# Two fused transformer blocks: PSUM pairs from two pools, an earlier scaling of x, and two modulation vectors summed on VectorE

## The chip, the core and the metric

The kernel runs on one core of a Trainium2 chip. The metric is device time in microseconds (us), the median of several runs. One more execution of the same program was taken with the hardware profiler; all rows below are from it.

## The reference

The input x has 256 tokens of 2048 features. It goes through two blocks, each with a conditioning vector c. All arithmetic is to float32 accuracy.

```python
# block 1
mod = silu(c) @ w_ada + b_ada                       # six vectors of 2048: sh_m, sc_m, gt_m, sh_f, sc_f, gt_f
h = rmsnorm(x, pre_mix_norm) * (1 + sc_m) + sh_m
proj = h @ w_in                                     # HGRN2 (q, f, v, g) and gated DeltaNet (q, k, v, g, a, b) columns
y = concat(hgrn2(proj), gated_delta(proj)) @ w_out
x = x + gt_m * rmsnorm(y, post_mix_norm)
h = rmsnorm(x, pre_ffn_norm) * (1 + sc_f) + sh_f
y = square(relu(h @ w_ff1)) @ w_ff2
x = x + gt_f * rmsnorm(y, post_ffn_norm)
# block 2: the same frame with its own six vectors, four kinds of attention and a SwiGLU; then a last rms_norm
```

What matters here is the first lines: each of the six vectors of a block is one row of `silu(c) @ w_ada`, a product of a single row with a 2048x2048 slice of a weight matrix (16 MB), and the first product `h @ w_in` needs vectors 0 and 1, the second norm needs 3 and 4.

## The kernel before

**Weights.** Every weight arrives in items of 512 KB ("raw", 128x1024). ScalarE rounds an item to the reduced float32r format (wh), VectorE (in some later stages GpSimd) takes the rest (wl = raw - wh, L169 as all instructions, since a helper issues them), and TensorE multiplies the activations, split likewise into hTh and hTl, in three passes: h*wh, h*wl, l*wh. There are four slots for split items and five raw slots (eight in the early rounds). SyncE's queue issues the loads in the order of a list, `items`; an item is loaded when a raw slot comes free.

**Order.** The program is one straight list for each engine. Python code writes it with the help of a planner, `_Clock`, which adds up assumed costs for each instruction: `fill()` is called after each pair of k-tiles and issues evacuations (`pri`), modulation vectors (`urgent`), steps of the recurrences and of attention (`fillers`; not if VectorE's planned time is more than 12 us ahead of TensorE's) and the preparation of further items (`prep`).

**Modulation vectors.** The items of `ADA` lie between the weight items. There are two ways to do them. With `cg=True` (vectors 0 to 4 of block 1) TensorE does them: `ada_cg` takes two items, and four matmuls at a time write the four 32-row strips of one bank ("ada", 128*32 in the profile); ScalarE or VectorE takes the 128x512 bank over into an "acc" tile. The others (vector 5 of block 1, all of block 2) are done on VectorE: acc = raw * silu(c) + acc, with silu(c) as a scalar of each partition, 128x512 at a time, two for an item. `col_gen` then sums an acc over its partitions into columns A and B of a norm (AB["mix1"], AB["ffn1"], ...): in block 1 by matmuls with a column of ones, in block 2 by transposes and ScalarE sums. `row_gen` spreads a gate vector over all partitions. There are four acc tiles of 128x512; `room` forces waiting vectors out when they are taken.

**Start and early rounds.** First come the 16 items of the first quarter of vectors 0 and 1. Meanwhile x arrives, `x_pre` sums its squares, and `xnT_gen(q)` scales 512 columns on ScalarE, transposes them through TensorE and copies them by ScalarE. Then the first 12 k-tiles of the eight `wide` blocks (hq, hf, hv, hg, zq, zk, zv, gg of the first half) are done in three rounds of four k-tiles, since each quarter of vectors 0 and 1 opens four k-tiles of h (`first_hT`). hq and hf keep their two PSUM banks ("g", four banks) over all rounds. The six others take a pair of the pool "mx" (three banks) in each round, and it is emptied into SBUF partial sums (hv, hg and "part") after each: in round one by ScalarE and VectorE, then by `add_acc` on VectorE. `xnT_gen(1)` to `(3)` follow the first three blocks of round one. The rest of the projections with the recurrences (`hg_gen`, `gd_gen`), vectors 3, 4 and 2 and the output projection (oA, oB) come after.

The evacuation of the second half's hq waits until the first half's `hg_gen` is done, and that of the second half's zq, zk and zv until the first half's `gd_gen` is.

Of the kernel before, what the change touches and what calls it, by code (L numbers as in the profile page):

```python
# [9 lines left out]
F32 = mybir.dt.float32  # L10
# [9 lines left out]
D = 2048  # L20
# [158 lines left out]
def two_blocks(ctx, tc, I, out):  # L179
# [21 lines left out]
    accp = ctx.enter_context(tc.tile_pool(name="acc", bufs=4))  # L201
# [35 lines left out]
    def add_ada(blk, v, q, kp, fin, row, cg):  # L237
        items.append({"ada": (blk, v, q, kp), "fin": fin, "row": row, "cg": cg})

    def room(n):  # L240
        for _ in range(40):
            if len(accs) + n > 4:
                fill_step(True, urgent)

    def dma_to(n):
        while st["d"] < min(n, len(items)) and rslots:
# [5 lines left out]
            if "ada" in it:  # L252
                blk, vs, q, kp = it["ada"]
                c0 = vs[0] * D + q * 512
                w = adas[blk][0]
                if kp == 0 and (it["row"] or not it["cg"]):
                    room(len(vs))
                    for v in vs:
                        a = accp.tile([128, 512], F32, name="acc", tag="acc")
                        accs[blk, v, q] = a  # L260
                        if it["row"]:
                            pool.memset(a, 0.0)
                            sync.dma_start(a[0:1, :], adas[blk][1][c0:c0 + 512].rearrange("(o n) -> o n", o=1))
                if len(vs) == 1:
                    src = w[kp * 256:(kp + 1) * 256, c0:c0 + 512].rearrange("(k p) n -> p k n", p=128)
                else:
                    src = w[kp * 128:(kp + 1) * 128, vs[0] * D:(vs[1] + 1) * D].rearrange("p (v n) -> p v n", v=2)[:, :, q * 512:(q + 1) * 512]
# [6 lines left out]
    def prep(low=None):  # L274
# [9 lines left out]
        if "ada" in it:  # L284
            blk, vs, q, kp = it["ada"]
# [34 lines left out]
    def ada_cg(it):  # L320

        blk, (v,), q, kp = it["ada"]
        cgs.setdefault("held", []).append(it)
        if kp % 2:
# [3 lines left out]
            for j in range(4):  # L328
                i = cgs["held"][j // 2]
                kt = blk * 16 + 2 * i["ada"][3] + j % 2  # L330
                mm(p[32 * j:32 * j + 32], csil[:, kt:kt + 1].to_broadcast([128, 32]),
                   i["raw"][:, (j % 2) * 512:(j % 2 + 1) * 512], kp == 1, kp == 7)
# [4 lines left out]
        if kp == 7:  # L337
            if it["row"]:
                a = accs[blk, v, q]
                dve.scalar_tensor_tensor(a, p, 1 / 32, a, op0=MUL, op1=ADD)  # L340
            else:
                room(1)
                a = accs[blk, v, q] = accp.tile([128, 512], F32, name="acc", tag="acc")
# [352 lines left out]
    def col_gen(blk, v, q):  # L696
        a = accs.pop((blk, v, q))
        name = (("mix1", "ffn1"), ("mix2", "ffn2"))[blk][v // 3]
        p = mx()
        if blk == 0:  # L700
# [20 lines left out]
    def row_gen(blk, v, q, key, mul):  # L721
# [5 lines left out]
        a = accs.pop((blk, v, q))  # L727
# [20 lines left out]
    def ada_vecs(blk, vs, key=None, mul=False, cg=False):  # L748
        n = 8 * len(vs)
        for q in range(4):  # L750
            for kp in range(n):
                fin = None
                if kp == n - 1:
                    if key is None:
                        fin = lambda q=q: urgent.extend((clk.wr[clk.key(accs[blk, v, q])][0] + 0.2, col_gen(blk, v, q)) for v in vs)
                    else:
                        fin = lambda q=q: urgent.append((clk.wr[clk.key(accs[blk, vs[0], q])][0] + 0.2, row_gen(blk, vs[0], q, key, mul)))
                ADA.append((blk, vs, q, kp, fin, key is not None, cg))
# [1588 lines left out]
```

## Time and profile before

| | us |
|---|---|
| median of 3 runs | 2887.93 |
| lowest and highest | 2885.76, 2890.27 |
| the profiled execution | 2885.77 |
| its span, first to last instruction | 2883.8 |

The profile counts, for every engine, the time in which it executes ("busy"), and for each wait the instruction that ended it. PE is TensorE, PEld its weight loads (they overlap matmuls), DVE VectorE, ACT ScalarE, POOL GpSimd, SP SyncE. PEclk is TensorE's granted clock as a share of full speed. A matmul's duration in the profile includes a tail that the next matmul overlaps. In this execution the early rounds run from about 39.8 to 283 us (with bounds near 125 and 205), the projections with vectors 3 and 4 to about 540, the rest of the first block's mixer to about 865, its feed-forward to 1510, and the second block's mixer from about 1660 to 2165.

### The profile page before, as it was taken

What the parts mean: (1) busy time and instruction counts of PE and PEld (TensorE: products, weight loads), DVE (VectorE), ACT (ScalarE), POOL (GpSimd) and SP (SyncE); (2) the same over time, 40 slices, a digit from 0 to 9 for tenths busy, and PEclk for the clock granted to TensorE, in tenths of its full rate; (3) what the DMA queues carried; (4) which work ended last, traced back from release to release, by engine and by line L of the source; (5) the groups of instructions that cost most, each with busy time, mean ns of one, the idle gap of its engine ahead of it and who ended that gap; (6) DMA issues with size and microseconds to landing.
All of it is one profiled execution on the core that took longest, in us unless ns stands there. A gap on an engine that the chain in (4) does not pass through costs nothing.

```text
span 2883.8 us, 44820 instructions
## 1 busy us (share of the span) xinstructions
PE 2713.4 (94%) x17761; PEld 2377.2 (82%) x17761; DVE 1783.3 (62%) x2228; ACT 1246.2 (43%) x1963; POOL 464.1 (16%) x306
## 2 busy tenths in 40 slices
PE   6988999999979999999998899998979999999998
PEld 3666788877869899897997798886769989998997
DVE  1443563655568877778765657677866665554456
ACT  3322354344554444444444436454454443443443
POOL 1000123123040000000002465554520000000001
PEclk8998999999989999999999899999989999999999
DMA  9876775684548888988865675667747777656654
GB/s 337 241 210 194 206 254 181 209 270 147 167 142 295 310 292 296 317 279 296 296 211 168 180 216 166 199 207 239 252 144 233 232 237 236 187 184 193 183 183 146
DMA packets 346594, 643.93 MB, mean 223 GB/s; under 512 B 31488, under 2 KB 50640, under 8 KB 344976
## 3 DMA queue, kind: packets, MB, share of 16 engines
q1 hardware_dynamic: 343296, 628.26, 68.0%
q10 hardware_dynamic: 2336, 10.42, 0.9%
q8 instruction: 139, 2.28, 0.3%
q0 software_dynamic: 752, 2.39, 0.2%
q14 instruction: 71, 0.58, 0.1%
HBM read 636.27 MB, written 4.19 MB: 222 GB/s over the span
## 4 chain that ended last, share of the span: by engine, by line
PE 52%; DVE 7%; DMA 5%; issue 3%; ACT 3%; POOL 2%; SPq 0%; ACTq 0%; POOLq 0%; DVEq 0%
PE g L169 50%; DMA raw<-in_w_ff_dram 3%; PE mx L169 3%; DVE acc L169 2%; DVE wl L169 2%; ACT wh L169 1%; DMA raw<-in_ada_w_dram 1%; POOL wl L169 1%; DVE xres L169 1%; POOL y L169 1%; DMA raw<-in_w_in_dram 0%; DVE S L169 0%; ACT sq L169 0%; DVE y L169 0%; ACT hTh L169 0%
## 5 line engine op out<-in xcount | busy, mean ns | idle before, releaser
L169 DVE TENSOR_TENSOR wl<-raw,wh 128x1024 fp32r<-128x1024 f32 x696 | 871.8, 1258 | 720.6 <-ACT wh L169 713.3
L169 ACT ACTIVATE wh<-raw 128x1024 fp32r<-128x1024 f32 (+2 forms) x817 | 846.5, 1044 | 1078.8 <-PE g L169 683.3
L169 PE MATMUL g<-hTh,wh 128*128 128x256 f32 x3328 | 959.0, 288 | 4.0 <-ACT wh L169 2.3
L169 PE MATMUL g<-hTh,wl 128*128 128x256 f32 x3328 | 945.2, 284 | 1.9 <-POOL wl L169 1.2
L169 PE MATMUL g<-hTl,wh 128*128 128x256 f32 x3328 | 944.0, 284 | 0.3 <-DVE hTl L169 0.3
L169 PEld LDWEIGHTS g<-hTh,wh 128*128 128x128 f32 x3328 | 637.8, 192 | 42.9 <-issue 36.0
L169 PEld LDWEIGHTS g<-hTl,wh 128*128 128x128 f32 x3328 | 640.0, 192 | 1.9 <-DVE hTl L169 0.6
L169 PEld LDWEIGHTS g<-hTh,wl 128*128 128x128 f32 x3328 | 637.4, 192 | 3.0 <-POOL wl L169 1.7
L169 DVE SCALAR_TENSOR_TENSOR acc<-raw,csil,acc 128x512 f32<-128x512 f32 x432 | 391.9, 919 | 64.3 <-DMA raw<-in_ada_w_dram 57.7
L169 PE MATMUL g<-wh,rh 128*128 128x512 f32 x864 | 339.7, 393 | 0.0
L169 PE MATMUL g<-wh,rl 128*128 128x512 f32 x864 | 339.2, 393 | 0.0
L169 PE MATMUL g<-wl,rh 128*128 128x512 f32 x864 | 339.0, 392 | 0.0
L169 POOL TENSOR_TENSOR wl<-raw,wh 128x1024 fp32r<-128x1024 f32 (+3 forms) x121 | 275.8, 2288 | 236.4 <-ACT wh L169 232.3
L169 POOL TENSOR_TENSOR y<-y,gw 128x512 f32<-128x512 f32 x22 | 32.1, 1474 | 1308.1 <-ACT sq L169 749.9
L169 PEld LDWEIGHTS g<-wh,rl 128*128 128x128 f32 x864 | 162.6, 188 | 36.2
L169 PEld LDWEIGHTS g<-wl,rh 128*128 128x128 f32 x864 | 162.7, 188 | 35.7
L169 PEld LDWEIGHTS g<-wh,rh 128*128 128x128 f32 x864 | 162.6, 188 | 35.5
L169 PE MATMUL g<-wh,hTh 128*128 128x512 f32 (+3 forms) x344 | 136.5, 397 | 12.2 <-ACT hTh L169 12.2
L169 PE MATMUL g<-wl,hTh 128*128 128x512 f32 (+3 forms) x344 | 128.4, 373 | 2.5 <-POOL wl L169 2.5
L169 PE MATMUL g<-wh,hTl 128*128 128x512 f32 (+3 forms) x344 | 128.9, 375 | 0.1
L169 PE MATMUL ada<-raw,csil 128*32 128x512 f32 x640 | 107.7, 645 | 16.5 <-DMA raw<-in_w_ada_dram 14.7
L169 PEld LDWEIGHTS g<-wh,hTh 128*128 128x128 f32 x344 | 67.8, 197 | 35.9 <-ACT hTh L169 14.9
(460 smaller groups left out, 2762.5 us busy)
## 6 DMA issues: line engine op xcount, KB each, us to landing
raw<-in_w_ff_dram SPq DMA_DIRECT2D x256, 512.0 KB, 5.3
raw<-in_w_ada_dram SPq DMA_DIRECT2D x192, 512.0 KB, 5.0
raw<-in_ada_w_dram SPq DMA_DIRECT2D x192, 512.0 KB, 5.0
raw<-in_w_in_dram SPq DMA_DIRECT2D x176, 512.0 KB, 5.8
raw<-in_ffn_w_gate_dram SPq DMA_DIRECT2D x88, 512.0 KB, 4.0
raw<-in_ffn_w_up_dram SPq DMA_DIRECT2D x88, 512.0 KB, 3.7
raw<-in_ffn_w_down_dram SPq DMA_DIRECT2D x88, 512.0 KB, 4.1
raw<-in_w_out_dram SPq DMA_DIRECT2D x60, 512.0 KB, 4.6
```

What stands on the lines that cost most here:

```text
L169: r = f(out, *a, **kw)
```

## The change

1. In the early rounds hf, too, is summed through SBUF (its partial sum lies in the tile of hk, which isn't used yet). The seven blocks with partial sums take their banks from "mx" and from "g" in turn.
2. x is scaled at once on VectorE, right after its norm (whose multiply-add moves from GpSimd to VectorE), and the transposes are copied by VectorE. The column loads and the first two `xnT_gen` stand between the last items of the first phase; the others follow hq and hf.
3. Vectors 3 and 4 of block 1 are no longer done on TensorE but on VectorE, and all sums on VectorE are 1024 wide: a pair of vectors' quarters, or two quarters of one vector. There are two acc tiles of 128x1024. The columns of vectors 3 and 4 come from transposes and ScalarE sums.

```diff
-    accp = ctx.enter_context(tc.tile_pool(name="acc", bufs=4))
+    accp = ctx.enter_context(tc.tile_pool(name="acc", bufs=2))
...
+    def new_acc(blk, vq, row):
+
+        for _ in range(80):
+            if len({n for _, n in accs.values()}) > 1:
                 fill_step(True, urgent)
+        st["acc"] = st.get("acc", 0) + 1
+        a = accp.tile([128, 1024], F32, name="acc", tag="acc")
+        if row:
+            pool.memset(a, 0.0)
+            c0 = vq[0][0] * D + vq[0][1] * 512
+            sync.dma_start(a[0:1, :], adas[blk][1][c0:c0 + 1024].rearrange("(o n) -> o n", o=1))
+        for h, (v, q) in enumerate(vq):
+            accs[blk, v, q] = a[:, h * 512:(h + 1) * 512], st["acc"]
+        return a
...
-            for k in range(2):
-                v, kt = (vs[0], 2 * kp + k) if len(vs) == 1 else (vs[k], kp)
-                a = accs[blk, v, q]
-                sc = csil[:, blk * 16 + kt:blk * 16 + kt + 1]
-                w = it["raw"][:, k * 512:(k + 1) * 512]
-                if kt == 0 and not it["row"]:
-                    dve.tensor_scalar(a, w, sc, None, op0=MUL)
-                else:
-                    dve.scalar_tensor_tensor(a, w, sc, a, op0=MUL, op1=ADD)
+            a = st["accs", blk, vq]
+            sc = csil[:, blk * 16 + k:blk * 16 + k + 1]
+            if k == 0 and not it["row"]:
+                dve.tensor_scalar(a, it["raw"], sc, None, op0=MUL)
+            else:
+                dve.scalar_tensor_tensor(a, it["raw"], sc, a, op0=MUL, op1=ADD)
...
-        if blk == 0:
+        if blk == 0 and v < 2:
             for k in range(4):
                 mm(p[:, k:k + 1], a[:, k * 128:(k + 1) * 128], ones[:, 0:1])
...
-    for v in (3, 4):
-        ada_vecs(0, (v,), cg=True)
+    ada_vecs(0, (3, 4))
     ada_vecs(0, (2,), "gt_m", True, cg=True)
...
-        rsq(r1, s2, 1.0 / D, 2, pool)
+        rsq(r1, s2, 1.0 / D, 2)
+        for q in range(4):
+            for t in range(2):
+                xc = x[:, t, q * 512:q * 512 + 512]
+                dve.tensor_scalar(xc, xc, r1[:, t:t + 1], None, op0=MUL)
 
     def xnT_gen(q):
         for k in (2 * q, 2 * q + 1):
-            if k % 2 == 0:
-                for t in range(2):
-                    xc = x[:, t, k * 256:k * 256 + 512]
-                    act.activation(xc, xc, AF.Copy, scale=r1[:, t:t + 1])
...
-            act.activation(xnT[:, 2 * k:2 * k + 2], p.rearrange("p (a b) -> p a b", a=2), AF.Copy)
+            dve.tensor_copy(xnT[:, 2 * k:2 * k + 2], p.rearrange("p (a b) -> p a b", a=2))
...
-    more_cols()
-    xnT_gen(0)
+        if i == 11:
+            more_cols()
+        if i in (13, 15):
+            xnT_gen((i - 13) // 2)
...
-    for b, o in zip(wide[2:], ("hv", "hg", "oh1", "ol1", "oh2", "ol2")):
+    for b, o in zip(wide[1:], ("hk", "hv", "hg", "oh1", "ol1", "oh2", "ol2")):
...
-                pts, b.first = mbanks(), 4 * q
+                pts, b.first = mbanks() if wide.index(b) % 2 else banks(), 4 * q
...
-            if q == 0 and b in wide[:3]:
-                xnT_gen(wide.index(b) + 1)
+            if q == 0 and b in wide[:2]:
+                xnT_gen(wide.index(b) + 2)
```

The loads of the sums on VectorE change with them: an item is now 128 rows of 1024 columns (of one vector, or 512 of each of two) instead of 256 rows of 512 where one vector is done. `ada_vecs` forms the groups accordingly; the order of the items of vectors 0, 1 and 2 is as before.

## Rows read from the trace of the kernel before

**Rows 1.** The page's first part: busy us, share of the span, instructions.
```profile
PE 2713.4 (94%) x17761; PEld 2377.2 (82%) x17761; DVE 1783.3 (62%) x2228; ACT 1246.2 (43%) x1963; POOL 464.1 (16%) x306
```

**Rows 2.** Windows by stage, all engines; the header names the columns.
```profile
core 0: us, PE busy (x) PEld busy (x) DVE busy (x) ACT busy (x) POOL busy (x), PEclk, DMA share, GB/s
39.80:125.00 85.20, 74.80 (x468) 55.27 (x469) 33.27 (x48) 34.45 (x46) 0.00 (x0) 0.94 0.83 249
48.00:72.00 24.00, 20.60 (x133) 13.13 (x126) 6.11 (x6) 9.07 (x12) 0.00 (x0) 0.93 1.03 350
125.00:205.00 80.00, 66.43 (x415) 51.50 (x414) 32.58 (x49) 21.78 (x26) 0.00 (x0) 0.91 0.75 224
205.00:283.00 78.00, 63.77 (x383) 49.93 (x382) 29.21 (x39) 19.90 (x22) 1.81 (x2) 0.89 0.69 210
283.00:540.00 257.00, 249.97 (x1760) 200.73 (x1759) 138.47 (x239) 111.74 (x220) 55.48 (x42) 0.99 0.69 214
336.00:408.00 72.00, 71.96 (x561) 61.10 (x561) 59.59 (x116) 35.09 (x67) 11.49 (x10) 1.00 0.73 239
283.00:790.00 507.00, 495.68 (x3384) 406.74 (x3384) 282.41 (x458) 216.40 (x415) 107.53 (x86) 1.00 0.64 204
865.00:1510.00 645.00, 638.39 (x4152) 583.06 (x4151) 497.39 (x582) 285.31 (x393) 0.00 (x0) 1.00 0.85 289
1660.00:2165.00 505.00, 455.79 (x3032) 401.96 (x3031) 362.10 (x471) 249.42 (x534) 255.40 (x133) 0.95 0.64 204
```

**Rows 3.** Waits of TensorE, 39.8 to 285 us: total, times, longest.
```profile
PE mx L169 <- DVE part L169: 13.7, 6, 2.3
PE mx L169 <- DVE hg L169: 8.2, 2, 4.1
PE mx L169 <- ACT x L169: 5.3, 4, 2.9
PE mx L169 <- DVE hv L169: 4.7, 2, 2.3
PE mx L169 <- ACT part L169: 2.5, 3, 0.8
PE mx L169 <- ACT hg L169: 1.8, 1, 1.8
```

**Rows 4.** Timeline, one block boundary of round two: start, duration, instruction.
```profile
167.05 0.28 PE L169 MATMUL mx<-hTh,wl 128*128 128x256 f32 x1
167.67 1.22 DVE L169 TENSOR_TENSOR wl<-raw,wh 128x1024 fp32r<-128x1024 f32 x1 [1.65 <-ACT wh L169]
168.81 1.28 DVE L169 TENSOR_TENSOR part<-mx,part 128x512 f32<-128x512 f32 x2
...
169.65 0.36 PE L169 MATMUL mx<-hTh,wh 128*128 128x256 f32 x1 [2.31 <-DVE part L169]
```

**Rows 5.** Timeline, end of the first phase.
```profile
34.24 0.33 PE L169 MATMUL mx<-c,x 128*128 128x128 f32 x1 [1.18 <-ACT x L169]
...
35.67 2.44 PE L169 MATMUL mx<-ones,acc 128*128 128x1 f32 x16
...
37.49 1.23 DVE L169 TENSOR_TENSOR wl<-raw,wh 128x1024 fp32r<-128x1024 f32 x1 [27.52 <-ACT wh L169]
```

**Rows 6.** Windows of tile ada, 283 to 540 us (without GpSimd's column).
```profile
283.00:540.00 257.00, 36.61 (x232) 5.49 (x232) 0.00 (x0) 4.77 (x8) 0.99 0.69 214
```

**Rows 7.** VectorE by form, 865 to 1510 us: busy us, mean ns.
```profile
L169 DVE TENSOR_TENSOR wl<-raw,wh 128x1024 fp32r<-128x1024 f32 x223 | 271.8, 1223 | 114.5 <-ACT wh L169 112.0
L169 DVE SCALAR_TENSOR_TENSOR acc<-raw,csil,acc 128x512 f32<-128x512 f32 x244 | 177.4, 747 | 8.4 <-DMA raw<-in_ada_w_dram 5.5 <-DMA raw<-in_w_ada_dram 0.6
...
L169 DVE TENSOR_TENSOR rl<-relu,rh 128x512 fp32r<-128x512 f32 x30 | 20.8, 692 | 21.0 <-ACT rh L169 21.0
```

**Rows 8.** VectorE by form, 1660 to 2165 us.
```profile
L169 DVE SCALAR_TENSOR_TENSOR acc<-raw,csil,acc 128x512 f32<-128x512 f32 x127 | 164.7, 1297 | 54.8 <-DMA raw<-in_ada_w_dram 52.2
```

**Rows 9.** Waits of TensorE, 1660 to 2165 us.
```profile
PE mx L169 <- DVE S L169: 16.0, 12, 4.3
```

More of the change, by code (lines that the diff above doesn't have):

```diff
@@ L235, in add_w, with add_ada @@
         return len(items) - 1
[L237 to L242, printed above, removed]
-                fill_step(True, urgent)
+    def add_ada(blk, vq, k, fin, row, cg):
+        items.append({"ada": (blk, vq, k), "fin": fin, "row": row, "cg": cg})
+    def new_acc(blk, vq, row):
+        for _ in range(80):
+            if len({n for _, n in accs.values()}) > 1:
+                fill_step(True, urgent)
+        st["acc"] = st.get("acc", 0) + 1
[7 more added lines that the diff above has]
+        return a
     def dma_to(n):
@@ L252, in dma_to @@
             if "ada" in it:
-                blk, vs, q, kp = it["ada"]
-                c0 = vs[0] * D + q * 512
+                blk, vq, k = it["ada"]
+                v, q = vq[0]
+                c0 = v * D + q * 512
                 w = adas[blk][0]
[L256 to L265, printed above, removed]
-                else:
-                    src = w[kp * 128:(kp + 1) * 128, vs[0] * D:(vs[1] + 1) * D].rearrange("p (v n) -> p v n", v=2)[:, :, q * 512:(q + 1) * 512]
+                if it["cg"]:
+                    if k == 0 and it["row"] and q % 2 == 0:
+                        new_acc(blk, [(v, q), (v, q + 1)], True)
+                    src = w[k * 256:(k + 1) * 256, c0:c0 + 512].rearrange("(k p) n -> p k n", p=128)
+                else:
+                    if k == 0:
+                        it["acc"] = new_acc(blk, vq, it["row"])
+                        st["accs", blk, vq] = it["acc"]
+                    if vq[0][0] == vq[1][0]:
+                        src = w[k * 128:(k + 1) * 128, c0:c0 + 1024].rearrange("p (k n) -> p k n", k=2)
+                    else:
+                        src = w[k * 128:(k + 1) * 128, v * D:(v + 2) * D].rearrange("p (v n) -> p v n", v=2)[:, :, q * 512:(q + 1) * 512]
                 sync.dma_start(raw.rearrange("p (k n) -> p k n", k=2), src)
@@ L320, in ada_cg @@
     def ada_cg(it):
-        blk, (v,), q, kp = it["ada"]
+        blk, ((v, q),), kp = it["ada"]
         cgs.setdefault("held", []).append(it)
@@ L338, in ada_cg @@
             if it["row"]:
[L339 removed]
+                a = accs[blk, v, q][0]
                 dve.scalar_tensor_tensor(a, p, 1 / 32, a, op0=MUL, op1=ADD)
             else:
[L342 to L343 removed]
+                if v % 3 == 0:
+                    new_acc(blk, [(v, q), (v + 1, q)], False)
+                a = accs[blk, v, q][0]
                 act.activation(a, p, AF.Copy, scale=1 / 32)
@@ L748, in ada_vecs, with fin @@
     def ada_vecs(blk, vs, key=None, mul=False, cg=False):
[L749 to L758, printed above, removed]
+        if cg:
+            groups = [((v, q),) for q in range(4) for v in vs]
+        elif len(vs) == 2:
+            groups = [tuple((v, q) for v in vs) for q in range(4)]
+        else:
+            groups = [((vs[0], q), (vs[0], q + 1)) for q in (0, 2)]
+        for vq in groups:
+            def fin(vq=vq):
+                for v, q in vq:
+                    at = clk.wr[clk.key(accs[blk, v, q][0])][0] + 0.2
+                    urgent.append((at, col_gen(blk, v, q) if key is None else row_gen(blk, v, q, key, mul)))
+            n = 8 if cg else 16
+            for k in range(n):
+                ADA.append((blk, vq, k, fin if k == n - 1 else None, key is not None, cg))
     def rsq(dst, src, scale, n, eng=dve):
@@ L1941, in two_blocks @@
                 while ai < ntot and (ai - a0) < na * done / tot:
-                    for _ in range(1 + ADA[ai][6]):
+                    for _ in range(1 + ADA[ai][5]):
                         add_ada(*ADA[ai])
```

15 lines of the change are left out of this document (7 added, 8 removed).

## The prediction

> **What bounds the kernel now.** I read the busy times first: TensorE's matmuls are busy for 94% of the span, and VectorE comes next with 62% [rows 1]. So time can only come out of two things: TensorE's own work, and the holes in it. The windows by stage say where the holes are [rows 2]. From 39.8 to 283 us, the three early rounds, TensorE has 205.0 us of work in 243.2 us, at a granted clock of 0.94, 0.91 and 0.89 of full speed. From 283 to 540 it is full (249.97 of 257), likewise from 865 to 1510 (638.39 of 645). From 1660 to 2165 there are holes again (455.79 of 505). The change touches all four stretches, so each gets its own answer.
>
> In the early rounds the waits of TensorE name the cause [rows 3]. Five rows (part, hg and hv by VectorE, part and hg by ScalarE) are waits for a PSUM pair to be emptied: 13.7 + 8.2 + 4.7 + 2.5 + 1.8 = 30.9 us. One more, 5.3 us, is a wait for the scaling of x. One block boundary shows how it goes [rows 4]: the last matmul of a block starts at 167.05; VectorE first does a wl that is ahead in its queue (167.67), then adds the two banks to their partial sums (168.81, 1.28 us for both), and only at 169.65 does the next block start, 2.31 us late. The pool "mx" has three banks and every block wants two, so two blocks in a row can't overlap.
>
> **The change, part by part.**
>
> *PSUM pairs in turn.* wide[1] (hf) becomes a block that is summed through SBUF, and the seven such blocks take their pairs from "mx" and from "g" alternately. The next block then has a free pair when the last one ends, and the 1.28 us of adding runs under its matmuls. I take 28 of the 30.9 us as gone. It costs VectorE or ScalarE three more evacuations (round one's copy, two adds) and a last add, about 1.3 us each time by the same row, inside rounds in which VectorE is busy for some 40% [rows 2]; nothing for TensorE. Lower bound: half, 15 us, if a pair then waits for wl or data; upper, all 30.9.
>
> *Clock.* After such a hole the matmuls run at the lower of the two levels (1.2 against 2.4 GHz) for a while; that is the 0.91 and 0.89 in [rows 2]. In rounds two and three TensorE is busy for 66.43 + 63.77 = 130.2 us at about 0.90. If half of the missing tenth comes back, that is 130.2 x 0.05 = 6.5; I take 6 (bounds 0 and 13).
>
> *x and its transposes.* Scaling x leaves ScalarE and is done at once on VectorE, which has nothing to do until 37.49 (idle for 27.52 us before it) [rows 5], so its wait for the norm holds up nothing behind it. The transposes of the first quads and the column loads move between the ada matmuls of the first phase. That takes away the 5.3 us [rows 3] and, in the start-up, the stretch from the end of the last ada matmul to the "ones" matmuls at 35.67, of which 34.24 to 35.67 and the wait of 1.18 before it are x's [rows 5]: about 3 us. Against it, the copies of the transposes now stand in VectorE's queue behind wl, and the two after hq and hf can wait for a bank: I put 3 us. Net 5.
>
> Early rounds together: 28 + 6 + 5 = **39 us less** (bounds 15 and 52).
>
> *The feed-forward's vectors leave TensorE.* Vectors 3 and 4 are 64 items, 256 of the "ada" matmul records. Between 283 and 540 stand 232 records with 36.61 us [rows 6], so 256 are about 40 us; some of it is tail under the next matmul, I take 38. Together with the waits for their data (about 4; their rows are in the same stretch, and I take them for no more than that) and 2 for columns that are now transposes, TensorE alone would gain 44 us.
>
> VectorE gets 64 sums of 128x1024. The trace has none of that shape. From 512 to 1024 columns a two-input operation goes from 692 to 1223 ns, and the 512-wide sum takes 747 where GpSimd is idle [rows 7]: 747 + 531 = 1278 ns. Lower bound 1223, the 1024-wide row; upper, two 512-wide ones where GpSimd is busy, 2 x 1297 = 2594 [rows 8]. GpSimd is busy for 55.48 of the 257 us here [rows 2], against 255.40 of 505 in the slow rows, so I stay near the lower end: 1350 ns, 64 x 1.35 = 86 us.
>
> Does VectorE have room? From 283 to 540 it has 138.47 us of work [rows 2]; with 86 and the late add, 226. TensorE would have 250 - 40 = 210. VectorE's share was at most 0.83 where it was fullest (59.59 of 72, 336 to 408) [rows 2]; at that share 226 us take 272: 15 us *longer* than now. But work can slide: over 283 to 790 VectorE has 282.41 + 88 = 370, and at 0.83 that needs 446 us, less than TensorE's 507 - 44 = 463. So the ends are 15 us lost (nothing slides) and 44 won (all slides). The sums come in the order of the weight items and can't slide; what can is the recurrences' work, each step of which waits for the step before. Middle: **14 us less**.
>
> The rows show one thing that speaks against it: the same 512-wide sum takes 747 ns with GpSimd idle and 1297 with GpSimd at half load [rows 7, 8]. The Trainium skill (SBUF — State Buffer, "Who interferes with whom") says why that would be: a VectorE instruction with two SBUF inputs and a GpSimd one that reads SBUF shut each other out for a whole instruction. The trace agrees as far as these two means go. By that rule the stretch would hold VectorE's work and GpSimd's one after the other, 138.5 + 82 + 55.5 = 276 us, 19 longer than now, where my sum has 14 less.
>
> *The other vectors.* The 448 sums of the later vectors become 224 of double width, each pair 1494 - 1278 = 216 ns cheaper. From 865 to 1510 that buys nothing, since TensorE has 6.6 us of holes there [rows 2]. From 1660 to 2165 there are 127 of them [rows 8], some 63 x 0.22 = 14 us of VectorE's 362; the largest row of waits for VectorE's small work there is 16.0 us [rows 9], and 14/362 of such waits is under 1. I take 2 less (bounds 5 less, 3 more: a sum twice as long also stands longer before a short step).
>
> *At nothing.* Half as many bias rows and memsets for the sums, each twice as long, on SyncE's and GpSimd's queues; DMA bytes are the same; one tensor_scalar goes from GpSimd to VectorE while that idles. The two 1024-wide buffers hold what four 512-wide held, so SyncE waits for a buffer as before. Were that cover gone (a sum late, its buffer kept), the next item's load would be late, and raw slots behind it; that is in the third rival.
>
> **Sum.** 39 + 14 + 2 = 55 us. The profiled execution took 2885.77 us (span 2883.8); the median of the runs is 2887.93, 2.2 above it. 2887.9 - 55 = **2833 us**.
>
> **Rivals.**
> 1. *VectorE is the bound from 283 to 540 and nothing slides.* For it: 226 us at the best share shown is 272. Against it: the share after 540 is low. 39 - 15 + 2 = 26 less: 2862 us.
> 2. *TensorE alone sets that stretch.* For it: it is full there now, and VectorE idles for 118 of the 257 us. 39 + 44 + 2 = 85 less: 2803 us.
> 3. *GpSimd and VectorE get in each other's way, and the recurrences are late for the second half's blocks* (their evacuation waits until the first half's state is done). This is slower than before. Place: 283 to 540. With 1.73 us for each sum and nothing sliding, (139.9 + 64 x 1.73) / 0.83 = 302 us, 45 more than now, and the early gain is eaten: from there on it decides. At 2.0 us it is 323, 66 more: 2887.9 - 41 + 66 = 2913 us. For it: rows 8. Against it: GpSimd's load is less than half of that in rows 8.
> 4. *The change doesn't do what it says in the early rounds,* because the next wait comes right behind: the loads. From 125 to 283 they run at 210 to 224 GB/s, and the core reached 350 [rows 2], so 80 us x 224 / 350 = 51 us is the floor of a round that I expect at (243 - 36) / 3 = 69. If the loads' order leaves only 10 us of the 39: 2887.9 - 10 - 14 - 2 = 2862 us.
> 5. *VectorE and GpSimd take turns.* Where VectorE's own work, 64 sums of 1278 ns and GpSimd's work from 283 to 540 never overlap, the stretch takes 138.5 + 82 + 55.5 = 276 us, 19 more: 2887.9 - 41 + 19 = 2866 us. For it: the two means in rows 7 and 8. Against it: the weight splits (wl), which have two SBUF inputs too, would then be slowed as much, and in rows 8 GpSimd's share was 0.5, here 0.22. This is what the Trainium skill's page and section named above would make of it.
>
> **How the numbers follow.** My forecast 0.42, its own range 2815 to 2850. Rivals 1, 2, 4 and 5: 0.13, 0.20, 0.08 and 0.07. Rival 3 has 0.10, of which some 0.03 stops within 0.2% (6 us, about what a measurement of this kernel can tell from no change) and 0.07 is slower. Faster is the rest, 0.90. The range reaches a little past rivals 2 and 5: 2795 to 2870; it leaves out rival 3 and the far ends of the others, under 2 in 10.
>
> **What would show it.** Right: in the early rounds the waits for part, hg and hv are under 5 us together, the granted clock is above 0.95, and the rounds end some 35 to 45 us earlier (part one). From there to the end of the fourth block of oA the distance shrinks by 5 to 25 us; the 1024-wide sums take 1.28 to 1.4 us there; VectorE's share is near 0.8 and TensorE has new waits for wl or for the recurrences' tiles (part two). After that, stage lengths are as before to within 5 us. Wrong: new waits of TensorE for raw or wl in the early rounds (rival 4); sums near 2 us and holes of TensorE between 300 and 540 (rival 3); a stretch with no new waits and 40 us less (rival 2).

## The result, and the profile after

The changed kernel takes 2815.6 us (median of 4 runs, 2811.03 to 2820.7) where the kernel before, on the same chip, takes 2889.1 (2885.76 to 2900.01): a ratio of 0.9738, 95% interval 0.9713 to 0.9762. The forecast was 2833. The profiled execution took 2814.65 us, its span is 2812.9.

The first part of the page for the kernel after, to be laid beside [rows 1]:

```profile
PE 2658.8 (95%) x17473; PEld 2360.9 (84%) x17473; DVE 1786.1 (63%) x2093; ACT 1240.8 (44%) x2004; POOL 476.2 (17%) x296
```

TensorE has 54.6 us less work, and VectorE as much as before. Where the 71 us of span went is seen from marks that both traces have. In us, lengths of the stretches between them (hq: evacuation of a half's hq; y: the first evacuation of oA), each from the one profiled execution:

| | to the first g matmul | to the first hq | to the second hq | to y | feed-forward of block 1 | second mixer (last relu to the end of the first up) | the rest |
|---|---|---|---|---|---|---|---|
| before | 39.8 | 245.7 | 125.1 | 324.2 | 629.6 | 681.0 | 838.4 |
| after | 36.8 | 184.3 | 177.7 | 280.2 | 622.9 | 671.8 | 839.2 |

So the start and the early rounds gave 64.4 us, where I had 39. The stretch of vectors 3 and 4, from the first hq to y, *lost* 8.6 (449.3 to 457.9), where I had a gain of 14; within it 52.6 are lost until the second hq, and 44.0 come back behind it. The later stages gave 15.1, where I had 2. Not all of the 64.4 belong to the first two parts: *e4_34_on_pe* below, without the move of vectors 3 and 4, has its first hq at 229.7 us, the kernel after at 221.1, so 8.6 of them come with the move.

The windows of the kernel after, by stage (same columns as [rows 2]):

```profile
36.80:104.50 67.70, 67.18 (x454) 51.01 (x455) 35.22 (x49) 27.77 (x35) 0.00 (x0) 0.97 0.98 324
104.50:160.00 55.50, 55.50 (x386) 44.09 (x385) 30.87 (x51) 20.11 (x24) 0.00 (x0) 1.00 0.97 301
160.00:218.00 58.00, 58.00 (x408) 49.53 (x407) 35.36 (x45) 19.69 (x22) 2.88 (x2) 1.00 0.86 268
218.00:399.00 181.00, 144.20 (x993) 131.45 (x991) 144.49 (x212) 71.00 (x172) 37.65 (x27) 0.89 0.68 203
264.00:360.00 96.00, 78.57 (x604) 74.63 (x603) 94.76 (x145) 41.46 (x98) 17.14 (x10) 0.96 0.75 228
362.00:386.00 24.00, 13.12 (x67) 10.43 (x67) 11.90 (x23) 8.50 (x33) 13.27 (x13) 0.73 0.37 122
386.00:410.00 24.00, 21.89 (x97) 18.94 (x97) 6.70 (x10) 12.68 (x29) 7.87 (x6) 0.63 0.15 44
809.00:1450.00 641.00, 638.48 (x4171) 584.65 (x4171) 476.54 (x456) 287.65 (x395) 0.00 (x0) 1.00 0.85 291
1597.00:2095.00 498.00, 453.36 (x3058) 399.15 (x3057) 310.70 (x407) 250.02 (x535) 264.43 (x129) 0.96 0.65 208
```

The three early rounds (first three lines) are now full: 180.68 of 181.20 us, at a granted clock of 0.97, 1.00 and 1.00. From 264 to 360 the roles are exchanged: VectorE has 94.76 us of work in 96, TensorE 78.57. And from 362 to about 400 little gets done: TensorE is busy for 13.12 of 24 us and then, with no more than 97 matmul records, for 21.89 (the granted clock is 0.73 and 0.63), VectorE has 11.90 and 6.70 of 24, and the loads all but stop (122 and 44 GB/s).

TensorE's waits after, 36.8 to 218 us. These are all that are left beside [rows 3]:

```profile
PE g L169 <- ACT hTh L169: 1.4, 1, 1.4
PE g L169 <- DVE hTl L169: 0.5, 1, 0.5
```

and from 218 to 410 us, with the two longest of SyncE's queue in the same stretch:

```profile
PE g L169 <- DVE wl L169: 13.3, 11, 4.1
PE mx L169 <- DVE gdT L169: 7.9, 1, 7.9
PE g L169 <- ACT wh L169: 6.1, 2, 3.2
PE g L169 <- DVE hk L169: 3.4, 1, 3.4
...
SPq L169 <- DVE acc L169: 70.7, 31, 5.3
SPq L169 <- DVE wl L169: 53.9, 19, 36.1
```

Two things stand in it: TensorE waits for the splits (wl) of a full VectorE, and one load waits 36.1 us. The timeline shows what that long wait is:

```profile
362.18 0.28 PE L169 MATMUL g<-hTh,wl 128*128 128x256 f32 x1
...
368.22 0.63 ACT L169 ACTIVATE oh<-hgA 128x512 fp32r<-128x512 f32 x1
...
376.81 1.11 PE L169 MATMUL mx<-c,gdT 128*128 128x128 f32 x4 [7.91 <-DVE gdT L169]
...
377.95 1.26 POOL L169 TENSOR_TENSOR ol<-hgA,oh 128x512 fp32r<-128x512 f32 x1
...
398.35 1.08 ACT L169 ACTIVATE hq<-g 128x512 f32<-128x512 f32 x2
...
400.23 0.77 PE L169 MATMUL g<-wh,hTh 128*128 128x512 f32 x1
```

At 362.18 the second half's hq and hf are multiplied and hold all four banks of "g". Their evacuation waits in the order for the end of the first half's hg_gen. Its last results are written at 368.22 and 377.95, but the evacuation stands on ScalarE behind steps of gd_gen that the planner put ahead of it, a chain in which each waits for the one before (gdP, gdT, gdG). The next matmul with weights starts at 400.23.

### The profile page after: what moved, and what is told of

Read it like the earlier page. It is cut to its first block, busy times and chain, and to the rows that moved or that the text cites. A ratio compares the mean times of both kernels' runs of the same rounds, so it can differ in the third digit from the quotient of the medians.

```text
span 2812.9 us, 44136 instructions
## 1 busy us (share of the span) xinstructions
PE 2658.8 (95%) x17473; PEld 2360.9 (84%) x17473; DVE 1786.1 (63%) x2093; ACT 1240.8 (44%) x2004; POOL 476.2 (17%) x296
## 5 line engine op out<-in xcount | busy, mean ns | idle before, releaser
L169 PE MATMUL g<-hTh,wh 128*128 128x256 f32 x3376 | 971.9, 288 | 9.5 <-ACT wh L169 8.1
L169 PE MATMUL g<-hTh,wl 128*128 128x256 f32 x3376 | 961.2, 285 | 16.4 <-DVE wl L169 12.6
L169 PE MATMUL g<-hTl,wh 128*128 128x256 f32 x3376 | 958.3, 284 | 0.5 <-DVE hTl L169 0.5
L169 PEld LDWEIGHTS g<-hTh,wh 128*128 128x128 f32 x3376 | 647.5, 192 | 36.3 <-issue 23.6
L169 PEld LDWEIGHTS g<-hTh,wl 128*128 128x128 f32 x3376 | 646.8, 192 | 20.3 <-DVE wl L169 15.0
L169 DVE SCALAR_TENSOR_TENSOR acc<-raw,csil,acc 128x1024 f32<-128x1024 f32 x276 | 381.6, 1383 | 81.4 <-DMA raw<-in_ada_w_dram 78.2
L169 PE MATMUL g<-wh,hTh 128*128 128x512 f32 (+3 forms) x368 | 147.0, 399 | 16.0 <-ACT hTh L169 12.6
L169 PE MATMUL g<-wl,hTh 128*128 128x512 f32 (+3 forms) x368 | 139.8, 380 | 4.2 <-POOL wl L169 2.6
L169 PE MATMUL g<-wh,hTl 128*128 128x512 f32 (+3 forms) x368 | 139.2, 378 | 0.0
L169 PEld LDWEIGHTS g<-wl,hTh 128*128 128x128 f32 x368 | 72.8, 198 | 15.8 <-POOL wl L169 4.1
```

The costliest lines, as they stand in the source:

```text
L169: r = f(out, *a, **kw)
```

## The experiments

Each time is a median of several runs, each ratio is to the kernel before, timed on the same chip, with its 95% interval (it need not be the quotient of the two medians). Stretches are from the one profiled execution of each kernel.

**Parts one by one.** First the three parts, each by itself on the kernel before.

*e1_pairs*, part one alone:

```diff
-    for b, o in zip(wide[2:], ("hv", "hg", "oh1", "ol1", "oh2", "ol2")):
+    for b, o in zip(wide[1:], ("hk", "hv", "hg", "oh1", "ol1", "oh2", "ol2")):
...
-                pts, b.first = mbanks(), 4 * q
+                pts, b.first = mbanks() if wide.index(b) % 2 else banks(), 4 * q
```

> The kernel before with the first part alone: hf is summed through SBUF and the seven blocks take their PSUM pairs from both pools in turn. Theory A (the pairs cost more than their 30.9 us of waits, because each hole also cost the clock): first matmul of hq to evacuation of hq falls from 245.7 us to 190 to 200, granted clock there 0.97 or more, and the whole kernel is 45 to 60 us faster than before. Theory B (the prediction's sizes: 28 for waits, 6 for the clock): 34 us faster, the stretch near 212. Theory C (the early gain of the changed kernel came mostly from x's scaling and start-up): under 20 us faster.

2841.19 us, ratio 0.9827 (0.9812 to 0.9843). The stretch to the first hq falls from 245.7 to 203.5, the others stay within some 3 us. The length is a little above what theory A expects and the clock (0.96) a little below, the time, 49 less, in its range. None of the five rows of waits for a pair [rows 3] is left. Its window:

```profile
39.60:241.00 201.40, 191.74 (x1264) 146.60 (x1265) 97.99 (x139) 76.64 (x94) 1.80 (x2) 0.96 0.89 277
```

Over the early rounds the kernel before had 38.2 us of holes (243.2 - 205.0 [rows 2]), this one 9.7: 28.5 less, the 28 of the forecast. TensorE's work for the same blocks is 13.3 us less, at a clock of 0.96 in place of 0.94, 0.91 and 0.89: the upper bound of the clock's term (13), not the 6 that I took.

*e2_x*, part two alone: the scaling (its hunk is shown with e8_scale_only), the places (shown with e11_place) and the copies:

```diff
-            act.activation(xnT[:, 2 * k:2 * k + 2], p.rearrange("p (a b) -> p a b", a=2), AF.Copy)
+            dve.tensor_copy(xnT[:, 2 * k:2 * k + 2], p.rearrange("p (a b) -> p a b", a=2))
```

> The kernel before with the second part alone: x scaled at once on VectorE, transposes copied by VectorE, column loads and two transposes moved into the first phase. Prediction's size: 5 us faster (first matmul of hq 3 us earlier, waits for x gone, new waits for copies up to 3). Theory C above: 20 us or more faster.

2875.9 us, ratio 0.9937 (0.9916 to 0.9958): about 14 less by the medians, 18 by the ratio. The start-up is 3.0 shorter and the stretch to the first hq 11.8. I had 5 for all of it.

*e3_vectors*, part three alone, with `new_acc` and all that goes with it:

```diff
-    for v in (3, 4):
-        ada_vecs(0, (v,), cg=True)
+    ada_vecs(0, (3, 4))
```

> The kernel before with the third part alone: vectors 3 and 4 on VectorE, all sums 1024 wide. The prediction's sizes: 14 + 2 = 16 us faster. What the stage marks of the changed kernel suggest instead: evacuation of hq to first evacuation of oA 5 to 10 us longer, feed-forward 5 to 7 shorter, second mixer 5 to 10 shorter, so 0 to 10 us faster in all. If VectorE were hopelessly full there: slower.

2884.15 us, ratio 0.9984 (0.9971 to 0.9998): some 5 us less, hardly clear of no change. The stretch from the first hq to y is 460.4, 11.1 *longer* than before, split as in the kernel after (178.6 and 281.8); the second mixer is 674.9 in place of 681.0 and the feed-forward 626.5 in place of 629.6. The loss is thus of part three itself, not of early rounds that end sooner.

**What part two consists of.** Two more, on the kernel before: *e8_scale_only* takes the scaling to VectorE and leaves the transposes' places and their copies on ScalarE; *e11_place* moves the transposes and column loads and leaves scaling and copies on ScalarE.

```diff
-        rsq(r1, s2, 1.0 / D, 2, pool)
+        rsq(r1, s2, 1.0 / D, 2)
+        for q in range(4):
+            for t in range(2):
+                xc = x[:, t, q * 512:q * 512 + 512]
+                dve.tensor_scalar(xc, xc, r1[:, t:t + 1], None, op0=MUL)
...
-            if k % 2 == 0:
-                for t in range(2):
-                    xc = x[:, t, k * 256:k * 256 + 512]
-                    act.activation(xc, xc, AF.Copy, scale=r1[:, t:t + 1])
```

> The kernel before with only the scaling of x put at once on VectorE (and the norm's multiply-add with it); the transposes stay where they were and are copied by ScalarE. If the scaling is what the second part of the change is worth, the waits for x (5.3 us) go and the time falls by about 5 to 8 us, to 2880 to 2885 us. If the place of the transposes (between the last items of the first phase, and off ScalarE's queue) is worth more, most of the 12 to 18 us that the second part gave by itself stays out and the time is 2884 to 2890 us.

```diff
-    more_cols()
-    xnT_gen(0)
+        if i == 11:
+            more_cols()
+        if i in (13, 15):
+            xnT_gen((i - 13) // 2)
...
-            if q == 0 and b in wide[:3]:
-                xnT_gen(wide.index(b) + 1)
+            if q == 0 and b in wide[:2]:
+                xnT_gen(wide.index(b) + 2)
```

> The kernel before with only the places changed: the column loads and the first two groups of transposes between the last items of the first phase, the others after hq and hf; x is still scaled on ScalarE and the copies are ScalarE's. If the place is what the second part gave (14 us, of which the scaling alone gave at most 4), the time is 2874 to 2880 us. If place and scaling are only worth something together, because ScalarE's scaling stands in front of the splits of items at the new place, it is 2884 to 2895 us.

2885.46 us, 0.9983 (0.9966 to 1.0), and 2885.06 us, 0.9994 (0.9978 to 1.0011). Neither alone gives what both give together. In e8_scale_only the waits for x are gone, the start-up is 2.0 us shorter and the rounds are not (245.4); e11_place reaches the first hq 2.4 us earlier than before. e2_x reaches it 14.8 us earlier: some 10 us come only with the copies on VectorE, or with all three together. ScalarE's longest waits from 36 to 112 us, in e8_scale_only:

```profile
ACT wh L169 <- PE mx L169: 18.5, 8, 3.3
ACT xnT L169 <- PE mx L169: 8.2, 3, 7.0
```

and in e2_x:

```profile
ACT wh L169 <- DMA raw<-in_w_in_dram: 20.3, 9, 4.3
ACT wh L169 <- PE mx L169: 13.7, 5, 3.6
```

The window of that stretch, e8_scale_only and e2_x:

```profile
36.00:112.00 76.00, 66.41 (x415) 49.66 (x415) 31.07 (x45) 28.69 (x38) 0.00 (x0) 0.91 0.84 263
```

```profile
36.00:112.00 76.00, 72.12 (x482) 53.76 (x482) 37.85 (x61) 30.09 (x39) 0.00 (x0) 0.98 0.98 311
```

In e8_scale_only ScalarE's copy of a transpose (xnT) waits up to 7.0 us for TensorE, which does the transposes at the end of a block, and the splits (wh) of the next items stand behind it. In e2_x these copies are VectorE's, and ScalarE waits for the loads instead. The same wait stands in the kernel before and in e11_place (6.4 and 7.4 us at the longest).

That these late splits, and the loads behind them, held TensorE up is not shown. None of TensorE's own waits in that stretch names a split or a load of w_in. They sum to 10.2 us in e8_scale_only and to 4.6 in e2_x; what is gone in e2_x is mostly a wait for hg (1.8) and these two:

```profile
PE mx L169 <- ACT xnT L169: 1.8, 3, 0.7
PE ada L169 <- DMA raw<-in_w_ada_dram: 1.1, 1, 1.1
```

What the windows show is 5.7 us less of holes and a granted clock of 0.98 in place of 0.91, so that 482 matmul records fit in where 415 did. The loads (311 GB/s in place of 263) go up by about as much as TensorE's records, and can be cause or consequence. That the copies are the decisive piece is read from these rows; a kernel with the copies alone was not run.

**Where vectors 3 and 4 are done.** *e4_34_on_pe* is the kernel after with these two back on TensorE, the wide sums kept for all others.

```diff
-    ada_vecs(0, (3, 4))
+    ada_vecs(0, (3, 4), cg=True)
```

> The changed kernel with vectors 3 and 4 back on TensorE (one argument of one call); the 1024-wide sums of the other vectors stay. Theory D (the move was a loss in its own stretch, as VectorE is 0.97 busy there and TensorE waits): evacuation of hq to first evacuation of oA is no longer than the changed kernel's 457.9 us, probably near before's 449, and the kernel is 5 to 15 us faster than the changed one. Theory E (the move pays its 40 us of TensorE work, and the stretch would be longer still without it): 15 to 40 us slower than the changed one.

2812.73 us, ratio 0.9729 (0.9712 to 0.9746), against 0.9738 of the kernel after: the move is worth nothing, between theories D and E. Theory D has the stretch right: from the first hq to y it takes 448.5 us in place of 457.9. But the early rounds are 9.0 us longer with these vectors' matmuls in them, and that takes the gain back. Then half of the quarters on either engine, in three orders, and three quarters on TensorE (`qs` names the quarters):

```diff
-    ada_vecs(0, (3, 4))
+    ada_vecs(0, (3, 4), cg=True, qs=(0, 1))    # e6_half
+    ada_vecs(0, (3, 4), qs=(2, 3))
...
+    ada_vecs(0, (3, 4), qs=(0, 1))             # e7_half_first
+    ada_vecs(0, (3, 4), cg=True, qs=(2, 3))
...
+    ada_vecs(0, (3, 4), qs=(0,))               # e9_mid
+    ada_vecs(0, (3, 4), cg=True, qs=(1, 2))
+    ada_vecs(0, (3, 4), qs=(3,))
...
+    ada_vecs(0, (3, 4), cg=True, qs=(0, 1, 2)) # e10_three
+    ada_vecs(0, (3, 4), qs=(3,))
```

> The changed kernel with quarters 0 and 1 of vectors 3 and 4 done first on TensorE, then quarters 2 and 3 on VectorE. Theory 'place': VectorE is only full while the first half's HGRN2 recurrence runs (it has 23.3 to 23.9 us of work in each 24 us there), so sums that come later are free: the stretch from the first hq to the second is 130 us or less in place of 178, the stretch after it 285 to 300, and the time 2790 to 2800 us, 15 to 25 less than the changed kernel. Theory 'amount': TensorE's work moved and VectorE's work moved offset each other wherever they stand; both stretches lie between those of the changed kernel and of the one with all of vectors 3 and 4 on TensorE (448 to 458 us together) and the time is 2808 to 2818 us.

> The same halves in the other order: quarters 0 and 1 of vectors 3 and 4 on VectorE, then quarters 2 and 3 on TensorE. Theory 'place': the sums stand where VectorE is full, so the stretch between the two evacuations of hq stays long (165 to 180 us) and the later one is not shortened as much as in the changed kernel; the time is 2815 to 2830 us, no better than the changed kernel. Theory 'amount': the same time as with the other order, to within 3 us.

> The changed kernel with quarters 1 and 2 of vectors 3 and 4 on TensorE, quarters 0 and 3 on VectorE: the sums stand before and after the stretch in which VectorE is full. By the theory 'place' this is the best order: no matmuls for vectors in the early rounds (185 us, as in the changed kernel), 130 to 145 us between the two evacuations of hq, 295 to 305 us after it, and 2785 to 2800 us in all. If it matters only how many sums VectorE has before the second hq (here 15 or 16, in the order VectorE first 30, in the order TensorE first almost none), the time lies between those two kernels: 2800 to 2808 us.

> Quarters 0 to 2 of vectors 3 and 4 on TensorE, quarter 3 on VectorE. If TensorE's own work sets the time where VectorE has room, 16 more items of vectors on TensorE than with the half cost it 64 matmuls of about 0.15 us, some 10 us: 2805 to 2812 us. If VectorE is still the bound after the second hq with half of the sums there, the time is the same as with the half, 2797 to 2803 us, or less.

| quarters on VectorE | time | ratio (interval) | to the first hq | to the second | to y | start to y |
|---|---|---|---|---|---|---|
| 0 to 3 (after) | 2815.6 | 0.9738 (0.9713, 0.9762) | 184.3 | 177.7 | 280.2 | 679.0 |
| none (e4_34_on_pe) | 2812.73 | 0.9729 (0.9712, 0.9746) | 193.3 | 131.0 | 317.5 | 678.2 |
| 3 (e10_three) | 2805.55 | 0.9718 (0.9694, 0.9742) | 193.0 | 128.6 | 305.7 | 664.2 |
| 2, 3 (e6_half) | 2799.71 | 0.9693 (0.9664, 0.9722) | 192.3 | 130.3 | 304.4 | 664.8 |
| 0, 1 (e7_half_first) | 2808.91 | 0.9727 (0.9698, 0.9756) | 185.1 | 157.5 | 292.5 | 671.6 |
| 0, 3 (e9_mid) | 2790.68 | 0.9660 (0.9635, 0.9684) | 184.6 | 139.1 | 294.0 | 654.2 |

The theory "place" holds by the stretches. Where VectorE has the sums while the first half's hg_gen runs (0 to 3; 0 and 1), the stretch to the second hq is long; where TensorE has matmuls for vectors before that (none; 3; 2 and 3), it costs 7 to 9 us in the early rounds, where TensorE is full. With quarter 0 early and 3 late there is little of either. The theory "amount" wants 448 to 458 us from the first hq to y wherever the sums stand; e6_half has 434.7 and e9_mid 433.1. e7_half_first alone (450.0 us, and 2808.91) would fit "amount" too, and there "place" missed: it is 9 us slower than the other order (the two intervals overlap), but its stretch is 157.5 where 165 to 180 were expected and its time below 2815 to 2830. e10_three, by its time, falls into its first case (2805 to 2812), but it and e6_half reach y together; what lies between them lies in later stretches, which neither edit touches, so it does not tell the cases apart. e9_mid is faster than either order of the halves (its interval overlaps that of e6_half), and its interval and that of the kernel after do not touch. The three windows of TensorE's work to y, for the kernel after and for e9_mid:

```profile
36.80:221.00 184.20, 183.68 (x1268) 147.62 (x1269) 103.87 (x146) 68.97 (x82) 2.88 (x2) 0.99 0.94 300
221.00:399.00 178.00, 141.20 (x968) 128.45 (x966) 142.06 (x211) 69.59 (x171) 37.65 (x27) 0.89 0.67 200
399.00:679.00 280.00, 273.09 (x1855) 230.55 (x1855) 180.72 (x267) 121.50 (x254) 69.49 (x54) 0.99 0.65 211
```
```profile
36.50:221.10 184.60, 184.23 (x1268) 148.20 (x1269) 104.03 (x146) 69.16 (x82) 2.87 (x2) 0.98 0.93 300
221.10:360.20 139.10, 128.13 (x934) 105.81 (x933) 107.33 (x171) 66.18 (x164) 21.89 (x18) 0.98 0.80 248
360.20:654.20 294.00, 290.43 (x2015) 244.93 (x2014) 174.66 (x275) 128.00 (x265) 79.74 (x62) 1.00 0.62 204
```

In the kernel after TensorE has 597.97 us of work in 642.2 (44.2 of holes), in e9_mid 602.79 in 617.7 (14.9). With all the quarters on TensorE it is 623.42 in 641.8 (18.4). How much of it is matmuls for vectors the sums over the same windows tell, for tile ada alone (the kernel after, e4_34_on_pe, e9_mid); the last two lines are all of TensorE's work in the kernel after and e4_34_on_pe:

```profile
sum 642.20, PE 50.42 PEld 7.74 DVE 2.73 ACT 3.59; mean PE 16.81 PEld 2.58 DVE 0.91 ACT 1.20
sum 641.80, PE 93.40 PEld 13.93 DVE 2.74 ACT 8.38; mean PE 31.13 PEld 4.64 DVE 0.91 ACT 2.79
sum 617.70, PE 70.73 PEld 10.36 DVE 2.72 ACT 5.97; mean PE 23.58 PEld 3.45 DVE 0.91 ACT 1.99
36.80:679.00 642.20, 597.97 (x4086) 506.63 (x4086) 426.65 (x622) 260.07 (x505) 110.02 (x82) 0.96 0.74 233
36.40:678.20 641.80, 623.42 (x4341) 501.36 (x4342) 350.69 (x558) 265.34 (x512) 102.01 (x82) 0.99 0.74 234
```

| first g matmul to y, us | vectors' matmuls | all others | holes | sum |
|---|---|---|---|---|
| all quarters on VectorE (after) | 50.4 | 547.6 | 44.2 | 642.2 |
| all on TensorE (e4_34_on_pe) | 93.4 | 530.0 | 18.4 | 641.8 |
| 0 and 3 on VectorE (e9_mid) | 70.7 | 532.1 | 14.9 | 617.7 |

So the move does take 43.0 us of vectors' matmuls off TensorE, and all of it is lost again: 25.8 us in new holes (net of 13.7 us of TensorE's waits for these vectors' loads, which fell from 15.6 to 1.9), and 17.5 because the other matmuls (3766 records and 3765) take 3% longer at a mean granted clock of 0.96 in place of 0.99 (0.89 from 221 to 399 us, where most of the holes are). e9_mid keeps half of the relief and has neither loss.

**Is it the hole, or the work?** *e12_free_hq* is the kernel after with nothing but the release moved: the evacuation of the second hq and hf is let go as soon as hg_gen's last reads of them are issued.

```diff
-            while half and g.get("hg_done") != 0:
+            while half and g.get("hg_free") != 0:
...
+            if tl:
+                g["hg_free"] = half
             yield from head_out(...)
...
     def ev_gate(key, after=None):
         def ev(pts):
+            while key == "hg" and g.get("hg_free") == 0 and g.get("hg_done") != 0:
+                yield
```

> The changed kernel, in which the evacuation of the second half's hq and hf is released as soon as the instructions of the first half's hg_gen that read hq and hf last have been issued (and only that of hg waits for its end), instead of at the end of hg_gen, whose last steps stand behind steps of gd_gen. Nothing is added or left out. Theory 'order': the hole before the second hq (362 to 400 us in the changed kernel) is made by the place of that evacuation in the order. The stretch to the second hq falls from 178 to 130 to 145 us, the one after it grows by less than half of that (280 to 300 us), and the time is 2790 to 2805 us. Theory 'work': VectorE's work up to there is the bound, and the hole only moves: the two stretches together stay at 450 to 458 us, and the time at 2810 to 2818 us.

2804.84 us, ratio 0.9701 (0.9685 to 0.9716). The hole is gone, the second hq comes at 135.9 us after the first, and the stretch behind it grows from 280.2 to 315.9: of 41.8 us 35.7 are lost again. Together the two are 451.8 us, 6.1 less than in the kernel after; another 5.5 us of the profiled difference lie in the second mixer (666.3), which this edit doesn't touch. So the time lies at the upper edge of the theory "order" (its interval just touches that of the kernel after), and the stretches are those of the theory "work": the hole is mostly where VectorE's lateness shows, and a small part of it (6 us) is the order's own. The window shows why:

```profile
264.00:360.00 96.00, 81.26 (x605) 77.81 (x604) 94.25 (x145) 42.91 (x101) 16.80 (x10) 0.91 0.75 225
```

VectorE is as full as without the edit (94.25 of 96).

**The width of the sums.** *e5_narrow* is the kernel after with every wide sum issued as two 512-wide ones on the same item.

```diff
+            for j in range(2):
+                aj, wj = a[:, j * 512:(j + 1) * 512], it["raw"][:, j * 512:(j + 1) * 512]
...
+                    dve.scalar_tensor_tensor(aj, wj, sc, aj, op0=MUL, op1=ADD)
```

> The changed kernel with each 1024-wide sum on VectorE issued as two 512-wide ones, on the same item, buffer and load. Where the width is not what shortens the later stages (the forecast's 2 us), the second mixer and the feed-forward stay as after (313 and 623 us, within 2) and the time is that of the changed kernel plus at most 5 us from the stretch with vectors 3 and 4: about 2816 to 2821 us. Where the width is what shortens them (the rival: 127 sums of 1297 ns became 64 of 1658 ns in the second mixer), the feed-forward grows by 4 to 7 us and the second mixer with attention by 5 to 16, and the time is 2826 to 2840 us.

2827.89 us, ratio 0.9786 (0.9759 to 0.9812): 12 slower than the kernel after, with intervals that just touch. From the first hq to y it loses 5.7 us, in the second mixer 8.3 (680.1), nothing in the feed-forward (622.4). VectorE's sums of the kernel after by form, from 218 to 400, 809 to 1450 and 1597 to 2095 us:

```profile
L169 DVE SCALAR_TENSOR_TENSOR acc<-raw,csil,acc 128x1024 f32<-128x1024 f32 x35 | 44.7, 1277 | 0.5 <-DMA raw<-in_w_ada_dram 0.4
...
L169 DVE SCALAR_TENSOR_TENSOR acc<-raw,csil,acc 128x1024 f32<-128x1024 f32 x122 | 156.0, 1279 | 2.3 <-DMA raw<-in_ada_w_dram 1.2 <-DMA raw<-in_w_ada_dram 0.6 <-DVE wl L169 0.3
...
L169 DVE SCALAR_TENSOR_TENSOR acc<-raw,csil,acc 128x1024 f32<-128x1024 f32 x64 | 106.1, 1658 | 77.3 <-DMA raw<-in_ada_w_dram 77.0
```

and of e5_narrow in the second mixer:

```profile
L169 DVE SCALAR_TENSOR_TENSOR acc<-raw,csil,acc 128x512 f32<-128x512 f32 x126 | 150.9, 1242 | 57.9 <-DMA raw<-in_ada_w_dram 57.8
```

126 sums of 1242 ns became 64 of 1658: 45 us less of VectorE's time there, 59 against the kernel before [rows 8]. TensorE's waits for VectorE's small work (S) in that stretch are 16.0 us before [rows 9], 15.6 in e5_narrow and 5.6 after. All runs agree on this stretch: the six kernels with 512-wide sums take 680 to 690 us for it, the eight with 1024-wide ones 666 to 675.

## Why the prediction was right, and where it was not

The direction and the range were right, the range in part by luck: only the first of the five terms had its size. The early terms gave 64.4 in place of 39 and the later stages 15.1 in place of 2, and the vectors' stretch, 8.6 lost in place of 14 won, took more than half of that excess away. The time is 2815.6, at the lower edge of the likeliest case's own range.

- **PSUM pairs: right.** 28 us of waits were forecast to go, 28.5 went (e1_pairs). The views that gave it, the waits by tile and one block boundary, were enough.
- **Clock: mis-sized.** 6 us were taken as the middle of 0 and 13; 13.3 came with the pairs alone (over all three rounds), and in the kernel after the granted clock is 1.00 in rounds two and three. The half that I took had no reason in any row; with the holes gone, about all of it came back.
- **x: mis-sized.** The wait of 5.3 us [rows 3] was counted and 3 set against it for copies behind wl. It measured 14 in the time (14.8 by the marks, 3.0 of them in the start-up). The scaling alone gave 2.3 us to the first hq and the places alone 2.4; the rest came only with the copies off ScalarE, and the wait of these copies for TensorE (up to 7.0 us) is in no row that I priced. By what path it costs TensorE the 10 us stays open; the rows show shorter holes and, with them, the clock, which this term left out.
- **Vectors 3 and 4: wrong in sign.** The step that failed is "Middle: 14 less", which assumed that half of the work slides. Measured the stretch is 8.6 longer (11.1 in e3_vectors); with the 8.6 that the move gave the early rounds it was worth nothing to y (679.0 us, 678.2 with the vectors back on TensorE). The durations in it were right (1277 ns measured, 1278 by the rows, 1350 taken), and so was TensorE's relief (43.0 us, 38 to 40 forecast). What it put at nothing is what TensorE lost for it: 25.8 us of holes, and 17.5 us of slower matmuls at a lower clock. The recurrence's steps were taken as what can slide, but the second half's hq waits for their end. VectorE can be fuller than 0.83 (94.76 of 96), which did not help, since the splits and hg_gen's steps then wait in its queue: hg_gen's last oh comes 147.1 us after the first hq, and 127.6 with the vectors on TensorE.
- **The later stages: mis-sized.** "2 less" became 15.1. In the second mixer it is the width (8.3 by e5_narrow, 9.2 between before and after): I priced a pair at the undisturbed 216 ns, while beside GpSimd's work a pair saves 2 x 1297 - 1658 = 936 ns. That price alone does not mend the term: scaled by VectorE's share as I did, 59 of 362 us would take 2.6 from the 16.0 us of waits for S, and 10.4 went. The feed-forward's 6.7 are not the width, for e5_narrow keeps them; over all kernels of this study that stretch lies between 622 and 631 us whatever the width, and what sets it stays open.

Of the signs that I named, those of part one came, stronger than stated. Of part two's the durations (1.28 us) and the new waits for wl came; the shorter distance to y did not, and VectorE's share was 0.99 where I had 0.8.

The rivals. Rival 1 (VectorE is the bound, nothing slides, 15 us lost) came nearest in the stretch of vectors 3 and 4, and its loss was hidden by the other two terms. Rival 2 (TensorE alone sets it) falls by the same rows. Rival 3 had the right place, a recurrence that is late and an evacuation that waits for it, and the wrong cause: the sums are not slowed (1277 ns) and the hole is paid back for the most part, so its 66 us never came. Rival 4 falls: no wait for raw in the early rounds, 268 to 324 GB/s. Rival 5 falls by its size: its 19 us were 8.6, and 9.4 against e4_34_on_pe. That VectorE's 94.76 and GpSimd's 17.14 us from 264 to 360, 111.9 together, lie in 96 does not speak against taking turns, as far as GpSimd's rough spans tell, since an instruction's span can hold its waiting, as the stretched ones here suggest: there VectorE's sums keep their 1271 to 1284 ns, and GpSimd's are the ones that stretch, up to 3.41 us where 1.15 is the shortest of the same shape (below). The rule of the Trainium skill that stood behind it (SBUF — State Buffer, "Who interferes with whom": two SBUF inputs on VectorE and a reading GpSimd exclude each other for a whole instruction) agrees with both stretches as far as these spans tell, with GpSimd waiting in the first and VectorE, up to 2.2 us a sum, in the second mixer (below). That the splits would be slowed as well was no argument against it: in the kernel before, wl takes 1553 ns in the mean from 1660 to 2165 us and 1223 in the feed-forward [rows 7]. What the rival had wrong is that the stretch must then hold both engines' work end to end.

## What to carry to other kernels

Before work is moved to an engine with a low mean share, look at its share in the very stretch, and at who is queued behind it there: here moving vectors from TensorE to VectorE was worth nothing (all quarters, 2812.73 to 2815.6) or 22 us (quarters 0 and 3, to 2790.68). A hole behind a late evacuation is a symptom: e12_free_hq took it away and kept 6 of 42 us, e9_mid moved the work and gained 25 in all. A hole costs more than its length: here 25.8 us of new holes came with 17.5 us of slower matmuls around them. When a step leaves a queue, look at what stood behind it in that queue, too.

## What the runs showed of the hardware

A sum with two SBUF inputs takes 746 to 747 ns (512 wide) and 1279 ns (1024 wide) where GpSimd is idle. Where GpSimd is busy for a fifth of the time the wide one keeps 1277, and the narrow one has 779 in the mean (e5_narrow); where GpSimd is busy for half of it, the means are 1242 to 1297 and 1658. But the mean is no sum's own time. VectorE's sums in the kernel after, from 218 to 400 and from 1597 to 2095 us (shortest, median and longest, in ns), and two of GpSimd's products in the first of these stretches (start and duration, in us):

```profile
L169 DVE SCALAR_TENSOR_TENSOR acc<-raw,csil,acc x35: 1271/1277/1284, 219.7 to 366.1; 128x1024 f32<-128x1024 f32 x35
L169 DVE SCALAR_TENSOR_TENSOR acc<-raw,csil,acc x64: 1266/1284/3417, 1601.3 to 2087.3; 128x1024 f32<-128x1024 f32 x64
...
300.61 3.41 POOL L169 TENSOR_TENSOR hk<-hk,hf 128x512 f32<-128x512 f32 x1 [15.82 <-PE mx L169]
...
324.94 1.15 POOL L169 TENSOR_TENSOR hk<-hk,hf 128x512 f32<-128x512 f32 x1 [5.85 <-PE mx L169]
```

Beside a half-busy GpSimd the median sum is not slowed, in the 512-wide kernels neither (752 ns before, 747 in e5_narrow), and the longest takes 2.1 to 2.2 us more than that at either width (3417, 2893 and 2957 ns). So the delay falls on some instructions and does not grow with their width, and half as many of them lose less than half: 64 x 0.38 = 24 us in place of 127 x 0.55 = 70. And a granted clock of 1.00 came where the short holes of some 2 us at block boundaries were gone, and 0.89 where new holes had come (221 to 399 us).
